# A decoder layer with 32 experts: tokens gathered for four experts at once, pairs combined by two-pass float32r products, and one branch moved

## The chip, the core and the metric

The kernel runs on one core of a Trainium2 chip. The metric is the time of one execution in microseconds (us); lower is better. TensorE (PE) multiplies matrices out of on-chip memory into PSUM, VectorE (DVE) and ScalarE (ACT) work element by element, GpSimd (POOL) does a few fills, and SyncE (SP) issues the transfers, which 16 DMA engines carry out.

## What is computed

One layer for 256 tokens of 1024 channels in float32. A token mixer with three groups of heads comes first, then a layer norm. After it come a mixture of experts, a gated embedding path, and a second layer norm:

```python
x = LN(alpha*x + mixer(x))
x = LN(alpha*x + MoE(x) + sigmoid(x W_g + b_g) * (p W_p))

logits = h @ w_router + b_router
top_v, top_i = lax.top_k(logits, 4)          # 4 of 32 experts for each token
gates = softmax(top_v)
gu = hb @ w_gate_up[e] + b_gate_up[e]        # hb: the tokens of expert e; 1024 -> 2048
g, u = min(gu[:, ::2], 7), clip(gu[:, 1::2], -7, 7)
act = (u + 1) * (g * sigmoid(1.702 * g))
y_e = act @ w_down[e] + b_down[e]            # 1024 -> 1024, added to the token, times its gate
```

Every expert's weights are read: 8 MB of w_gate_up and 4 MB of w_down each, 384 MB of the 431 MB that the kernel reads.

## The kernel before, in words

**The stream of weights.** SBUF has a ring of 22 slots of 1 MB (8 KB in each of 128 partitions, line 150). `want` queues units in the order of their use, `pump` gives a unit a slot as soon as one is free and issues its transfer from SP, and `done` frees a slot and pumps on. SP carries the transfers out in program order, so one that waits for a slot holds all that follow. An expert is 12 units: 8 of w_gate_up (`load_flat`, L245) and 4 of w_down (`load_rows2`, L224, for the last expert L231 and L239). Four slots are taken out of the ring for good (`room`, line 289: "act", "swi", "out", "acc"), and two more during experts 9 to 12, so that some 18 slots carry the stream.

**The mixer** (lines 264 to 940) fills the first 145 us. Its projections split float32 matrices exactly into two float32r parts (`split`, L406 and L407) and multiply the parts (L417 to L420, 256 columns a product; L788 to L790, 512 columns). The products of float32 operands elsewhere show as two records each. Its last part writes the normed stream `xn` (L861), finds each token's place among its expert's (`posm`, L918) and the gates `G` (`gates`, L924).

**The experts** (line 1271 on): one iteration e does up(e) and down(e - 1). Each expert has 64 slots for tokens. In an iteration, in the order of the code:

- the branch for more than 64 tokens at expert e (`over_up`, L1275), skipped by all experts but one;
- `expert_up(e)`: 32 float32 products of 512 columns (64 records, L1039), two blocks of columns side by side on the array; each row block of w_gate_up is released after use;
- the branch for the tokens past 64 of expert e - 1 (`over_down`, L1288), skipped likewise;
- at an even e `gather_gates` (L1003 to L1008): one-hots times gates, two transposes on TensorE, a copy; the result `CT` has the gates of two experts by slot and token;
- `expert_down(e - 1)` (32 records, L1066) into `y`, which holds a pair of experts in its two halves of partitions;
- `expert_act(e)`: copies out of PSUM (L1047, L1048), eight transposes (L1054) and the activation (`swiglu`, L1014 to L1020);
- at an even e `combine`: y of the finished pair times `CT`, four float32 products of 512 columns (8 records, L1028), each added to `yacc` by DVE (L1029);
- after it `gather` for the next pair: one-hots of posm (`Pm`, L986) multiplied with xn, 16 float32 products of 128 columns (32 records, L994), scaled out of PSUM in eight pieces by ACT and DVE (L966, L968) into `xe`, of which there are two buffers;
- in iterations 9 to 12 a quarter of the embedding path (`ple`, L1214 to L1226), which starts with 16 transposes of xn (L977);
- in iteration 4 `general()` (L1153): a branch for any counts, with loops inside. It is taken only above 96 tokens at an expert, and all engines skip it here.

The code's order is not quite the order of issue: within bounds each engine's list is ordered ahead of the run by readiness. After the last expert, its down runs by blocks of columns (`last_down`, L1336, and `last_combine`, L1345), and the second layer norm and the output follow.

Of the kernel before, what the change touches and what calls it, by code (L numbers as in the profile page):

```python
# [21 lines left out]
P = 128  # L22
# [19 lines left out]
GENERAL_AT = 4  # L42
NRUN = NE

# the table of shape constants: columns
# [11 lines left out]
# the packed small parameters: columns  # L57
# [49 lines left out]
def lay_out(inp):  # L107
    """The inputs as the launch takes them: small ones packed by partition, some transposed."""
# [18 lines left out]
    # ff = block * 256 + part * 128 + lane; column of w_gate_up = 2 * ff + (gate|up)  # L127
# [11 lines left out]
def kernel(ctx, tc, x, xT_in, pT_in, w_in, w_out, diff_lambda, params, bgu_in, w_gate_up,  # L139
# [9 lines left out]
    # ---- slots of 8 KB per partition: the stream of weights, and the mixer's larger intermediates  # L149
# [13 lines left out]
    def want(key, fn):  # L163
        pending.append((key, fn))

    def aside(fn):
        """fn() goes out in its place in the stream and takes no slot."""
        pending.append((None, fn))

    def pump():  # L170
        while pending and (free or pending[0][0] is None):
            key, fn = pending.pop(0)
            if key is None:
                fn()
                continue
            t, s = slot_tile()
            where[key] = s
            loaded[key] = fn(t)
# [28 lines left out]
    # ---- what the stream loads  # L207
# [56 lines left out]
    # ------------------------------------------------------------------ mixer  # L264
# [4 lines left out]
    def load_first_cols(u):  # L269
        """The first unit comes with xT, a quarter of each at a time."""  # L270
# [17 lines left out]
    # room that the experts need from then on, in places where the stream can spare it  # L288
    room = {3: "act", 5: "swi", 8: "out", 10: "acc"}
    n_want = RING  # L290
    for e in range(NRUN + 1):
# [20 lines left out]
        for key, fn in units:  # L312
            n_want -= 1
            if -n_want in room:
                key_ = room[-n_want]
                want(key_, lambda u: u)
# [60 lines left out]
    def keep_warm(n, warm, n_cols=512):  # L377
        """Products that nothing reads, so that the clock of the tensor engine stays up while it waits."""
# [21 lines left out]
    def split(half):  # L400
        """wh + wl = half of a unit exactly, each part with no more bits than a float32r has."""
# [46 lines left out]
    # output gates of groups A and C  # L448
# [12 lines left out]
    # ---- group A's gate of low rank: its 16 features in four parts, each the sum over a quarter of the channels  # L461
# [8 lines left out]
    # ---- group B's Toeplitz bias  # L470
# [12 lines left out]
    # ---- group A: gates, decays and scores of the gated linear attention  # L483
# [66 lines left out]
    # ---- group B: -lambda, scores and softmax  # L550
# [13 lines left out]
    def mixed(key, old, units):  # L564
        """Room for the high and low parts of two units of the mixed stream."""
# [21 lines left out]
    def diff_start(h, qz, kz):  # L587
        """A head's scores: each of its two maps has one half of the partitions."""
# [10 lines left out]
    def diff_softmax(h, t):  # L599
        """Both maps' weights of a tile of queries, and their difference."""  # L600
# [18 lines left out]
    def diff_turn(h, t):  # L619
        """The weights with keys along the partitions."""  # L620
# [7 lines left out]
    # ---- group C: retention scores  # L628
# [19 lines left out]
    def head_norm(o, po, blk, gcol):  # L648
        """o = po normed over a head's channels (po and o are channel by token)"""
# [31 lines left out]
    # ---- the rest of the projections, each group's work among those of the next  # L681
# [27 lines left out]
    # the router with the gain and bias of the layer norm: gain * w, and bias @ w + b  # L709
# [8 lines left out]
    # in each partition: -(the sum of an expert's weights), and its constant  # L718
# [54 lines left out]
    # expert e in each quarter of the partitions  # L773
# [3 lines left out]
    # ---- output projection, residual, first layer norm  # L777
# [24 lines left out]
    # xn is the normed stream without its gain and bias; x1T has both  # L802
    xn = cp.tile([P, NT, D], F32, name="xn")
# [3 lines left out]
    # the logits and four values above them all; the largest four, and four of those values  # L807
# [3 lines left out]
    nc.gpsimd.memset(lg[:, :, NE:], BIG)  # L811

# [458 lines left out]
    for e in range(NRUN + 1):  # L1271
# [10 lines left out]
        if e < 2:  # L1282
            bind(e)
# [103 lines left out]
```

## Time and profile before

| | |
|---|---|
| median of 3 runs (lowest to highest) | 1154.04 us (1151.01 to 1156.36) |
| span of the profiled execution, first to last instruction | 1148.8 us |
| TensorE, products | busy 1088.3 us, 95% |
| VectorE / ScalarE / GpSimd | 375.3 / 182.1 / 7.5 us (33% / 16% / 1%) |
| read from memory | 430.81 MB, 376 GB/s over the span |
| TensorE clock granted, mean | 0.981 |

The profile describes one execution, and this one's own time is its span; the median of the runs lies 5.2 us above the span, which holds what the runs have around it and their scatter. Busy time says how long an engine was in an instruction, not that it did its best. In a list of instructions over time, a line has the start, the length, the engine, the line of the kernel, the operation, output and input, the shape, a count, and in brackets how long the engine idled before and what ended that. An idle engine costs time only where its work is on the path to the end.

### The profile page before, as it was taken

What the parts mean: (1) busy time and instruction counts of PE and PEld (TensorE: products, weight loads), DVE (VectorE), ACT (ScalarE), POOL (GpSimd) and SP (SyncE); (2) the same over time, 40 slices, a digit from 0 to 9 for tenths busy, and PEclk for the clock granted to TensorE, in tenths of its full rate; (3) what the DMA queues carried; (4) which work ended last, traced back from release to release, by engine and by line L of the source; (5) the groups of instructions that cost most, each with busy time, mean ns of one, the idle gap of its engine ahead of it and who ended that gap; (6) DMA issues with size and microseconds to landing.
All of it is one profiled execution on the core that took longest, in us unless ns stands there. A gap on an engine that the chain in (4) does not pass through costs nothing. (4 is left out here: it accounts for less than half of the span.)

```text
span 1148.8 us, 14055 instructions
## 1 busy us (share of the span) xinstructions
PE 1088.3 (95%) x5566; PEld 548.7 (48%) x5566; DVE 375.3 (33%) x797; ACT 182.1 (16%) x372; POOL 7.5 (1%) x19
## 2 busy tenths in 40 slices
PE   9999999999699998999999999999998899999996
PEld 7888845434234344544534343434342433434334
DVE  4976632323023322411313132223232313222225
ACT  5457511101001111100101010101010100111001
POOL 1000000000000000000000000000000000000000
PEclk9999999999899999999999999999999898999999
DMA  9957888999799999999899999999999999999991
GB/s 319 361 220 265 336 344 338 405 402 416 302 416 417 416 407 407 398 360 388 331 416 416 415 415 417 415 416 416 416 415 417 416 417 417 393 417 416 415 347 38
DMA packets 100301, 433.64 MB, mean 377 GB/s; under 512 B 6957, under 2 KB 33325, under 8 KB 67409
## 3 DMA queue, kind: packets, MB, share of 16 engines
q1 hardware_dynamic: 100002, 431.36, 94.4%
q8 instruction: 90, 1.47, 0.5%
q0 software_dynamic: 176, 0.53, 0.1%
q14 instruction: 33, 0.27, 0.1%
HBM read 430.81 MB, written 1.06 MB: 376 GB/s over the span
## 5 line engine op out<-in xcount | busy, mean ns | idle before, releaser
L1039 PE MATMUL pgu<-u,xe 128*64 128x512 f32 x1024 | 242.1, 602 | 16.6 <-PEq L1288 9.9
L1039 PE MATMUL pgu<-u,u 128*64 128x512 f32 x1024 | 243.4, 604 | 5.8 <-PEq L1288 1.1
L1066 PE MATMUL py<-u,u 128*64 128x512 f32 x992 | 235.4, 602 | 5.7 <-DMA u<-in_w_down_dram 4.8
L1039 PEld LDWEIGHTS pgu<-u,xe 128*64 128x64 f32 x1024 | 85.5, 138 | 161.6 <-issue 149.7
L1039 PEld LDWEIGHTS pgu<-u,u 128*64 128x64 f32 x1024 | 89.7, 139 | 149.2 <-issue 139.0
L1048 DVE COPY u<-pgu 128x512 f32<-128x512 f32 x32 | 22.1, 692 | 392.9 <-PE pgu L1039 392.9
L1066 PEld LDWEIGHTS py<-u,u 128*64 128x64 f32 x992 | 80.6, 138 | 139.2 <-issue 121.7
L1014 DVE TENSOR_TENSOR u<-ptg,bgu 128x512 f32<-128x512 f32 x32 | 22.1, 692 | 219.8 <-PE ptg L1054 219.6
L1047 ACT COPY u<-pgu 128x512 f32<-128x512 f32 x32 | 18.8, 586 | 457.6 <-PE pgu L1039 457.6
L994 PEld LDWEIGHTS pgx<-Pm,xn 128*128 128x128 f32 x512 | 59.8, 192 | 8.3 <-issue 4.8
L994 PE MATMUL pgx<-Pm,xn 128*128 128x128 f32 x512 | 60.5, 275 | 1.0 <-PEq L1275 0.7
L1028 PE MATMUL pcb<-u,CT 128*128 128x512 f32 x120 | 57.5, 602 | 3.3 <-DVE u L1072 3.1
L1071 ACT COPY u<-py 64x512 f32<-64x512 f32 x31 | 17.9, 579 | 238.5 <-PE py L1066 238.5
L407 DVE TENSOR_TENSOR u<-u,u 128x1024 fp32r<-128x1024 f32 x32 | 39.1, 1223 | 17.1 <-ACT u L406 17.1
L1029 DVE TENSOR_TENSOR u<-u,pcb 128x512 f32<-128x512 f32 x64 | 43.5, 680 | 1.5 <-PE pcb L1028 1.5
L406 ACT CAST u<-u 128x1024 fp32r<-128x1024 f32 x32 | 33.5, 1048 | 29.9 <-PE pzt L418 9.6
L1028 PEld LDWEIGHTS pcb<-u,CT 128*128 128x128 f32 x120 | 20.6, 191 | 28.5 <-issue 14.1
L417 PE MATMUL pzt<-u,u 128*128 128x256 f32 x128 | 32.9, 291 | 0.0
L418 PE MATMUL pzt<-u,u 128*128 128x256 f32 x128 | 32.3, 287 | 0.0
L1214 PE MATMUL pleg<-u,u 128*128 128x256 f32 x128 | 29.8, 382 | 0.9 <-ACT u L1217 0.6
L1016 ACT ACTIVATE u<-u 128x512 f32<-128x512 f32 x32 | 20.2, 630 | 65.9 <-DVE u L1015 65.9
L1054 PEld LDWEIGHTS ptg<-ci,u 128*128 128x128 f32 x128 | 17.9, 207 | 26.3 <-issue 24.3
(277 smaller groups left out, 884.8 us busy)
## 6 DMA issues: line engine op xcount, KB each, us to landing
u<-in_w_gate_up_dram SPq DMA_DIRECT2D x256, 1024.0 KB, 16.7
u<-in_w_down_dram SPq DMA_DIRECT2D x127, 1024.0 KB, 17.6
u<-in_w_in_dram SPq DMA_DIRECT2D x11, 1024.0 KB, 12.9
u<-in_w_out_dram SPq DMA_DIRECT2D x4, 1024.0 KB, 11.0
u<-in_w_ple_gate_dram SPq DMA_DIRECT2D x4, 1024.0 KB, 17.8
u<-in_xT_dram SPq DMA_DIRECT2D x4, 256.0 KB, 4.1
u<-in_w_in_dram SPq DMA_DIRECT2D x4, 256.0 KB, 4.3
u<-in_w_in_dram SPq DMA_DIRECT2D x2, 512.0 KB, 7.2
```

The costliest lines, as they stand in the source:

```text
L406: nc.scalar.copy(wh, half)
L407: nc.vector.tensor_tensor(wl, half, wh.bitcast(F32), op=ALU.subtract)
L417: nc.tensor.matmul(pz[:, j, :], wh[:, k, :], xh[:, k, :], start=k == 0, stop=False)
L418: nc.tensor.matmul(pz[:, j, :], wh[:, k, :], xl[:, k, :], start=False, stop=False)
L994: nc.tensor.matmul(pg[:, j, :], xn[:, t, k * P:(k + 1) * P], Pm[:, t].rearrange("p e s -> p (e s)"), start=t == 0, stop=t == NT - 1)
L1014: nc.vector.tensor_tensor(g, pg, bg, op=ALU.add)
L1028: nc.tensor.matmul(pcb, CTp[:, t * P:(t + 1) * P], y[:, sl], start=True, stop=True)
L1029: nc.vector.tensor_tensor(yacc[:, t, sl], yacc[:, t, sl], pcb, op=ALU.add)
L1039: nc.tensor.matmul(pgu[b][hf * 64:(hf + 1) * 64, :], xe[:, k, c0:c0 + NSLOT], w[:, b * 1024 + hf * 512:b * 1024 + (hf + 1) * 512], start=k ...
L1048: nc.vector.tensor_copy(gs[:, 1, :], pgu[1])
L1066: nc.tensor.matmul(py[nb * 64:(nb + 1) * 64, :], act[:, j * 4 + blk, :], w[:, f % 2, nb * 512:(nb + 1) * 512], start=f == 0, stop=f == 7)
L1214: nc.tensor.matmul(pg[:, j, :], w[:, k, sl], x1T[:, k, :], start=k == 0, stop=k == NK - 1)
```

## The change

- `gather` works for groups: experts 0 and 1 as before, then four experts at a time (2 to 5, 6 to 9, ..., 26 to 29), and last 30 and 31. The one-hots are float32r; the normed stream is split once into `xnh` and `xnl` (float32r), and both are multiplied with the one-hots (256 columns a product). `xe` is one buffer for four experts. The gather of the next group stands after up(e) of a group's last expert.
- `gather_gates` stands ahead of expert_up(e) at an even e. It gives a one-hot `PT` (float32r) and a column `gate` in place of `CT`; the last pair keeps `CT`.
- `combine` of a pair becomes `weigh` (y times gate, split into `yh` and `yl`) in iteration e, and `combine_pair` (two float32r products for each of the four blocks) in iteration e + 1, after its up and gather. The combine in the branch and the last one stay.
- The transposes of `affine_transposed` become products of xnh and xnl with a float32r identity: 32 in place of 16.
- `xn` is `xs` normed in place; the slot of `xs` is freed after the split in iteration 0. `y` moves to the slot "swi", yh and yl take "out". The descriptor scratch of GpSimd's transfers shrinks from the default to 1024 bytes of a partition.
- `general()` goes from the end of iteration 4 to iteration 19, between the branch of expert 18 and down(18).

```diff
-GENERAL_AT = 4
+GENERAL_AT = 19
...
+    xnh = cp.tile([P, NT, D], F32R, name="xnh")
+    xnl = cp.tile([P, NT, D], F32R, name="xnl")
+    identr = cp.tile([P, P], F32R, name="identr")
+    nc.scalar.copy(identr, ident)
...
-            nc.scalar.activation(xn[:, t, sl], xs[:, t, sl], AF.Identity, scale=mv[:, 1:2], bias=nmr)
+            nc.scalar.activation(xs[:, t, sl], xs[:, t, sl], AF.Identity, scale=mv[:, 1:2], bias=nmr)
...
-                    nc.tensor.transpose(pt[:, k * P:(k + 1) * P], xn[:, t, (4 * q + k) * P:(4 * q + k + 1) * P], ident)
+                    ch = slice((4 * q + k) * P, (4 * q + k + 1) * P)
+                    for n, v in enumerate((xnh, xnl)):
+                        nc.tensor.matmul(pt[:, k * P:(k + 1) * P], v[:, t, ch], identr, start=n == 0, stop=n == 1)
...
+    def onehots(g):
+        n = size_of(g)
+        Pm = ep.tile([P, NT, n, NSLOT], F32R, name="Pm", tag="Pm", bufs=1)
+        sh = [P, NT, n, NSLOT]
...
+    def gather(g, Pm):
+        n = size_of(g) * NSLOT
+        w = 4 if g == 0 else 2
+        for q in range(NK // w):
+            pg = ps_s("pgx").rearrange("p (k s) -> p k s", k=w)
+            for j in range(w):
+                ch = slice((w * q + j) * P, (w * q + j + 1) * P)
+                for t in range(NT):
+                    hot = Pm[:, t].rearrange("p e s -> p (e s)")
+                    if g == 0:
+                        nc.tensor.matmul(pg[:, j, :n], xn[:, t, ch], hot.bitcast(F32), start=t == 0, stop=t == NT - 1)
+                        continue
+                    for i, v in enumerate((xnh, xnl)):
+                        nc.tensor.matmul(pg[:, j, :n], v[:, t, ch], hot, start=t + i == 0, stop=t + i == NT)
+            for j in range(w):
+                affine_evac(xe[:, w * q + j, :n], pg[:, j, :n], w * q + j, j % 2)
+
+    def split_stream():
+        for t in range(NT):
+            nc.scalar.copy(xnh[:, t], xn[:, t])
+            nc.vector.tensor_tensor(xnl[:, t], xn[:, t], xnh[:, t].bitcast(F32), op=ALU.subtract)
+        done("xs")
...
-        nc.vector.tensor_copy(CT, pct[:, :S])
-        return CT
+        if 2 * g + 2 == NRUN:
+            CT = ep.tile([P, S], F32, name="CT")
+            nc.vector.tensor_copy(CT, pct[:, :S])
+            return CT
+        PT = ep.tile([P, S], F32R, name="PT", tag="PT", bufs=2)
+        gate = ep.tile([P, 1], F32, name="gate", tag="gate", bufs=2)
+        nc.vector.tensor_scalar(PT, pct[:, :S], 0.0, None, op0=ALU.is_gt)
+        nc.vector.tensor_reduce(gate, pct[:, :S], axis=AX.X, op=ALU.add)
+        return PT, gate
...
+    def weigh(gate, y):
+        yh, yl = rm["yh"], rm["yl"]
+        for nb in range(2):
+            sl = slice(nb * 512, (nb + 1) * 512)
+            nc.scalar.activation(yh[:, sl], y[:, sl], AF.Copy, scale=gate)
+            nc.vector.scalar_tensor_tensor(yl[:, sl], y[:, sl], gate, yh[:, sl].bitcast(F32),
+                                           op0=ALU.mult, op1=ALU.subtract)
+        return yh, yl
+
+    def combine_pair(PT, ys):
+        yacc = rm["yacc"]
+        for t in range(NT):
+            for nb in range(2):
+                sl = slice(nb * 512, (nb + 1) * 512)
+                pcb = ps_s("pcb")
+                for i, v in enumerate(ys):
+                    nc.tensor.matmul(pcb, PT[:, t * P:(t + 1) * P], v[:, sl], start=i == 0, stop=i == 1)
+                nc.vector.tensor_tensor(yacc[:, t, sl], yacc[:, t, sl], pcb, op=ALU.add)
...
-            gs_of[e] = expert_up(e, st[e // 2][0])
+            if e % 2 == 0:
+                gates_of[e // 2] = gather_gates(e // 2, hot)
+            gs_of[e] = expert_up(e)
+        if e == 0:
+            split_stream()
+        if e + 1 < NRUN and group(e + 1) != group(e):
+            hot = onehots(group(e + 1))
+            gather(group(e + 1), hot)
         if e < 2:
             bind(e)
+        if weighed:
+            combine_pair(*weighed)
+            weighed = None
         if e == BIAS_AT:
             output_bias()
...
-        if e < NRUN and e % 2 == 0:
-            st[e // 2] = st[e // 2][0], gather_gates(e // 2, st[e // 2][1])
+        if e == GENERAL_AT:
+            general()
...
         if e >= 1 and f % 2 == 1:
-            combine(st.pop(f // 2)[1], y)
-        if (e == 1 or e % 2 == 0 and e > 0) and e + 2 < NRUN:
-            st[e // 2 + 1] = gather(e // 2 + 1)
+            PT, gate = gates_of.pop(f // 2)
+            weighed = PT, weigh(gate, y)
...
-        if e == GENERAL_AT:
-            general()
...
-    nc = bacc.Bacc("TRN2", target_bir_lowering=False, num_devices=1)
+    nc = bacc.Bacc("TRN2", target_bir_lowering=False, num_devices=1, dynamic_dma_scratch_size=1024)
```

## Rows read from the trace of the kernel before

**Rows 1.** The page's first part: busy time and share of TensorE's products and the others.

```profile
PE 1088.3 (95%) x5566; PEld 548.7 (48%) x5566; DVE 375.3 (33%) x797; ACT 182.1 (16%) x372; POOL 7.5 (1%) x19
```

**Rows 2.** Stretches: length, busy time of the engines, granted clock, DMA share, GB/s.

```profile
150.00:200.00 50.00, 48.27 (x235) 24.18 (x237) 12.89 (x28) 5.36 (x11) 1.81 (x1) 1.00 0.88 331
200.00:280.00 80.00, 77.12 (x346) 32.53 (x342) 20.32 (x37) 6.58 (x12) 0.00 (x0) 0.98 1.01 406
280.00:320.00 40.00, 29.86 (x140) 13.33 (x140) 8.52 (x19) 3.61 (x7) 0.00 (x0) 0.87 0.82 335
320.00:480.00 160.00, 154.58 (x729) 73.00 (x729) 48.78 (x96) 19.35 (x40) 0.00 (x0) 1.00 1.02 412
480.00:580.00 100.00, 93.41 (x420) 48.15 (x420) 21.42 (x39) 8.20 (x16) 0.00 (x0) 0.97 0.92 364
...
820.00:900.00 80.00, 71.42 (x315) 26.84 (x314) 18.04 (x35) 6.58 (x12) 0.00 (x0) 1.00 1.02 416
...
980.00:1000.00 20.00, 19.59 (x102) 10.30 (x99) 8.61 (x17) 3.04 (x6) 0.00 (x0) 1.00 0.96 384
1000.00:1100.00 100.00, 98.43 (x432) 40.33 (x429) 23.51 (x44) 11.35 (x20) 0.00 (x0) 0.98 1.02 416
1100.00:1120.00 20.00, 19.70 (x82) 7.50 (x82) 5.55 (x10) 0.59 (x1) 0.00 (x0) 1.00 0.96 320
```

**Rows 3.** TensorE in order of time, over one pair of experts (up 18 to up 20).

```profile
700.35 15.11 PE L1039 MATMUL pgu<-u,u 128*64 128x512 f32 x64
...
723.84 1.02 PE L1028 MATMUL pcb<-u,CT 128*128 128x512 f32 x2
725.12 2.81 PE L1028 MATMUL pcb<-u,CT 128*128 128x512 f32 x6 [0.26 <-DVE u L1072]
727.77 3.73 PE L994 MATMUL pgx<-Pm,xn 128*128 128x128 f32 x32
731.65 14.68 PE L1039 MATMUL pgu<-u,u 128*64 128x512 f32 x63
...
754.93 7.52 PE L1039 MATMUL pgu<-u,xe 128*64 128x512 f32 x34
```

**Rows 4.** The end: SP's last loads, and TensorE's next to last block of columns.

```profile
1109.38 5.68 SPq L239 DMA_DIRECT2D u<-in_w_down_dram  x2
...
1133.97 1.15 PE L1336 MATMUL pyl<-u,u 128*64 128x64 f32 x32
```

**Rows 5.** The mixer's float32r products in order of time: 256 columns, then 512.

```profile
20.43 0.28 PE L418 MATMUL pzt<-u,u 128*128 128x256 f32 x1
...
20.55 0.28 PE L417 MATMUL pzt<-u,u 128*128 128x256 f32 x1
...
121.04 0.39 PE L788 MATMUL pw<-u,u 128*128 128x512 f32 x1
...
121.27 0.39 PE L789 MATMUL pw<-u,u 128*128 128x512 f32 x1
```

**Rows 6.** TensorE, the first 12 of the embedding path's 16 transposes of xn.

```profile
429.72 1.85 PE L977 MATMUL ptx<-ci,xn 128*128 128x128 f32 x12
```

**Rows 7.** The mixer's splits by line: count, busy us, mean ns, idle before.

```profile
L407 DVE TENSOR_TENSOR u<-u,u 128x1024 fp32r<-128x1024 f32 x32 | 39.1, 1223 | 17.1 <-ACT u L406 17.1
L406 ACT CAST u<-u 128x1024 fp32r<-128x1024 f32 x32 | 33.5, 1048 | 29.9 <-PE pzt L418 9.6 <-DMA u<-in_w_in_dram 7.4 <-PE pw L789 6.1
```

**Rows 8.** TensorE after general() was skipped: up(5).

```profile
296.77 15.76 PE L1039 MATMUL pgu<-u,xe 128*64 128x512 f32 x64 [9.88 <-PEq L1288]
```

**Rows 9.** Experts 5 and 6: the last transposes, the activation's last step, the gates.

```profile
319.91 0.64 PE L1054 MATMUL ptu<-ci,u 128*128 128x128 f32 x4
...
324.24 0.69 DVE L1020 TENSOR_TENSOR u<-u,u 128x512 f32<-128x512 f32 x1
...
336.46 0.41 DVE L1008 COPY CT<-pct 128x256 f32<-128x256 f32 x1
...
336.79 0.42 DVE L1003 TENSOR_TENSOR Cm<-Pm,G 128x256 f32<-128x256 f32 x1
```

More of the change, by code (lines that the diff above doesn't have):

```diff
@@ L175, in pump @@
                 continue
-            t, s = slot_tile()
+            t, s = slot_tile(dtype)
             where[key] = s
@@ L315 @@
                 key_ = room[-n_want]
-                want(key_, lambda u: u)
+                want(key_, lambda u: u, F32R if key_ == 'out' else F32)
             want(key, fn)
@@ L910 @@
     done("m1")
-    done("xs")
+    xn = xs
     nc.tensor.matmul(ppos[:, 0:NE], tri, mb[:, 0, :], start=True, stop=True)
@@ L945 @@
     placed = [None]
-    xe0 = ep.tile([P, NK, 2 * NSLOT], F32, name="xe0")
+    xe = ep.tile([P, NK, 4 * NSLOT], F32, name="xe")
     def bind(e):
         if e == 1:
-            rm["y"], rm["yo"] = carve(loaded["out"], (D,), (D,))
+            rm["yh"], rm["yl"] = carve(loaded["out"], (D,), (D,))
             rm["yacc"] = loaded["acc"].rearrange("p (t d) -> p t d", t=NT)
@@ L980, in affine_transposed, with group @@
         return x1T
-    def gather(g):
-        Pm = ep.tile([P, NT, 2, NSLOT], F32, name="Pm", tag="Pm", bufs=1)
-        sh = [P, NT, 2, NSLOT]
-        placed[0] = nc.vector.tensor_tensor(Pm, iota[:, None, None, :NSLOT].to_broadcast(sh),
-                                            posm[:, :, 2 * g:2 * g + 2, None].to_broadcast(sh), op=ALU.is_equal)
-        xe = rm["xe1"] if g % 2 else xe0
-        for q in range(2):
-            pg = ps_s("pgx").rearrange("p (k s) -> p k s", k=4)
-            for j in range(4):
-                k = 4 * q + j
-                for t in range(NT):
-                    nc.tensor.matmul(pg[:, j, :], xn[:, t, k * P:(k + 1) * P],
-                                     Pm[:, t].rearrange("p e s -> p (e s)"), start=t == 0, stop=t == NT - 1)
-            for j in range(4):
-                affine_evac(xe[:, 4 * q + j, :], pg[:, j, :], 4 * q + j, j % 2)
-        return xe, Pm
+    def group(e):
+        return 0 if e < 2 else 1 + (e - 2) // 4
@@ L1080, in over_gather @@
             for t in range(NT):
-                nc.tensor.matmul(px[:, k, :NOVER], xn[:, t, k * P:(k + 1) * P], Po[:, t, :],
-                                 start=t == 0, stop=t == NT - 1)
+                for i, v in enumerate((xnh, xnl)):
+                    nc.tensor.matmul(px[:, k, :NOVER], v[:, t, k * P:(k + 1) * P], Po[:, t, :],
+                                     start=t + i == 0, stop=t + i == NT)
         xo = ep.tile([P, NK, NOVER], F32, name="xo", tag="xo")
@@ L1253, in broadcast_ln2 @@
             nc.scalar.copy(u[:, sl], pl)
-    st = {}
     y = None
-    st[0] = gather(0)
-    n_of = {}
+    hot = onehots(0)
+    gather(0, hot)
+    n_of, gates_of = {}, {}
     gs_of, act_of, ov_of = {}, {}, {}
+    weighed = None
     def count(e):
```

33 lines of the change are left out of this document (21 added, 12 removed).

## The prediction

> **What bounds the kernel now.** The first part of the page shows TensorE busy for 95% of the span and no other engine above 33% [rows 1]. That alone doesn't say that TensorE sets the time, so the second view is the table of stretches [rows 2], read from its last column: the reader is to see that the loads run at 416 GB/s wherever nothing holds them (820 to 900 us, 1000 to 1100) and never faster in a long stretch, and that the granted clock is 1.00 while TensorE waits for them (820 to 900). At 416 GB/s an expert's 12.58 MB take 30.25 us and a pair's 60.5 us. The third view is TensorE over one pair [rows 3]: from up(18) at 700.35 to up(20) at 754.93 us it works back to back, 54.6 us. So in the steady part TensorE is the quicker of the two, and the loads ought to set the pace.
>
> They don't from the start. At 150 us the ring is full, because the mixer used the loads more slowly than they came; a load then starts only when TensorE frees a slot, and each pause of TensorE is one of the stream. I count what the stream lost against 416 GB/s: 150 to 200 us (1 - 331/416) x 50 = 10.2 us; 200 to 280 1.9; 280 to 320 7.8; 320 to 480 1.5; 480 to 580 (the embedding path) 12.5; 980 to 1000 1.5 [rows 2]. Together 35.4 us, of which 25.2 after 200 us. In 1100 to 1120 us 6.4 MB were left, 15.4 us, so the stream ends near 1115.4; SP's last loads are issued at 1109.38 and landing fits [rows 4]. From there the kernel takes 33 us to its end at 1148.8, because TensorE has fallen behind again. The bound is thus mixed: the stream, its holes, which TensorE makes, and a tail on TensorE.
>
> **Gather, part by part.** One gather of a pair takes TensorE 3.88 us, from 727.77 to 731.65 [rows 3]. After gather(0), which stays, there are 15: 58.2 us. Afterwards there are 8, each of 32 products of 256 columns in float32r; the mixer's products of that shape follow each other by 0.12 us [rows 5], so 3.8 us each. The last one has 128 columns a product, which no row shows for float32r; the float32 gather's 32 records of 128 columns in 3.73 us bound it above at twice that, if each product costs two records, 7.5 us, and half of 0.12 us a product below, 1.9 us; I take 3.8. Sum 30.4, saved 27.8 us.
>
> **Combine.** It holds TensorE from 723.84 to 727.77, 3.93 us, a wait for y's copy included [rows 3]. 15 of them move to the new form: 59.0 us. Afterwards each has eight products of 512 columns at 0.23 us [rows 5]: 1.8 us, 27 in all, saved 32.0 us. It comes an iteration later, so the wait goes too. The Trainium skill (TensorE: Matmul & The Clock Gate, Back-to-back issue gap) gives about 131 ns for 512 columns in a sustained stream; a combine of 1.0 us is the estimate by that page. The row shows 0.23 us, and it decides.
>
> **Beside other work.** `weigh` adds two copies on ACT and two subtractions on DVE for each pair, about 0.7 us each (the 512-column step on DVE took 0.69) [rows 9], and has the 15 us of the next up to hide in [rows 3]; DVE is 33% busy [rows 1]. If that cover went, the combine would wait up to 2.8 us. The one-hot and the sum in place of one copy of 0.41 us add the like of one more such pass on DVE, with a whole up before they are needed. Eight pieces out of PSUM serve four experts instead of two, so ACT and DVE gain there. The split of the stream, two copies of 1.05 and two subtractions of 1.22 us [rows 7], runs on two engines beside up(0), a stretch like the 15 us of up(18) [rows 3]; without that cover it would hold gather(1) by up to 4.5 us. The slot of xs comes free later: at worst one load, 2.5 us of the stream, nothing at best, since the stream stands waiting there anyway (331 GB/s) [rows 2]; I take nothing. The transposes for the embedding path took 12 in 1.85 us, so 2.5 for 16 [rows 6]; 32 products cost between 1.9 and 7.5 us by the bounds above, and I take 0.12 each as for the 256 columns, since each needs a weight load of the same size: +1.3 us. The smaller scratch touches two small transfers in the mixer; I take nothing, and bound it by 2 us either way.
>
> **The branch.** Skipping general() leaves TensorE idle for 9.88 us [rows 8], at the end of iteration 4, when the ring is full: the stream loses 7.8 us there [rows 2]. At expert 19 the pause comes again. I take its TensorE time as the same 9.9 us, but let it cost the stream nothing, because TensorE then keeps up with the stream: the ring's 18 slots are 45 us of loads, and the pause fills a quarter of them. SP skips the branch too, with loads already issued in flight; a stream that stood as long as at expert 4 would cost 7.8 us, the upper end.
>
> **The sum.** TensorE gets 27.8 + 32.0 - 1.3 = 58.5 us less to do, 4 us a pair: 50.5 against the stream's 60.5. Up to up(5) alone it is ahead for good by the branch, 9.9, by one gather, 3.9, and by what one combine saves, 2.1: 15.9 us, so the hole at 280 to 320 us goes. Then it gains 10 us a pair on the stream until it waits for loads, and the embedding path, whose hole was 12.5 us in all, finds free slots. Of the 25.2 us I keep 3.0 (320 to 480 and 980 to 1000 us, the second after the branch of the one overfull expert). The stream ends at 1115.4 - 22.2 = 1093.2 us. TensorE, with 58.5 us less, is through up(31) by then, waiting for loads, and what is left after the last load is the next to last block and all behind it: 1148.8 - 1133.97 = 14.8 us [rows 4]. Span 1093.2 + 14.8 = 1108 us. The median of the runs shown is 5.2 us above the profiled span (1154.04 against 1148.8), so **1113 us**.
>
> **Rivals.**
> (A) This forecast, 1100 to 1122: at 1100 all 35.4 us of holes vanish (1115.4 - 35.4 + 14.8 + 5.2); at 1122 the branch costs the stream its 7.8 us and the unknown terms another one.
> (B) The stream doesn't end sooner. Where it ran at 416 GB/s, freeing TensorE brings nothing, and if the holes have other causes (code loading, SP's own order, the embedding path's loads), they stay: only the tail shrinks, 1115.4 + 14.8 + 5.2 = **1135 us**. For it: the stream is full in most stretches [rows 2]. Against it: the holes lie where TensorE paused or had extra work. The Trainium skill (Perfetto Trace Analysis, Identifying the Most-Contended Engine) says that busy time of matmuls is a bad measure, that the loads are judged by their rate, and that the most contended resource is the one to work on; by that rule this change turns the wrong screw, which is this case. The trace agrees in the steady part and not before 320 us.
> (C) A float32r product costs half of a float32 one, as one of its two records does: eight products of 0.43 us are 3.4 us a combine, 32 of 0.24 are 7.5 us for a gather of four. TensorE saves only half a microsecond a pair, and the time stays within 0.5%, near **1150**. Against it stand the mixer's 0.12 and 0.23 us [rows 5].
> (D) Slower: `gather_gates` now stands ahead of up(e), and on DVE its first step, one-hots times gates (`Cm`), stands behind the activation of the expert before. If it is issued there, TensorE idles from the end of the transposes (319.91 + 0.64) to the end of the activation (324.24 + 0.69) and 0.42 for the step: 4.8 us [rows 9], at 15 pairs 72 us, with everything in up(e) queued behind. A pause also lowers the clock: 0.87 over the stretch around the branch [rows 2], where up(5) took 15.76 against 15.11 us [rows 8, 3]; 15 times 0.65 is 9.8. 1148.8 + 72 - 58.5 + 9.8, less the 8.6 us that TensorE waited for loads in 820 to 900 [rows 2], is 1163.5 and with 5.2 **1169 us**. It decides from 3.9 us a pair on (58.5 over 15). Against it: `Cm` of the pair to come was issued 0.33 us after the copy of the pair before [rows 9], two iterations ahead of its place in the code, since its inputs are there; the same can happen now.
>
> **How the numbers follow.** A 0.64, B 0.20, C 0.07, D 0.09. Likeliest is A, 1113 us. The range runs from 1099 to 1140 and holds A and B with a few microseconds for their unknown terms; it leaves out 0.16. A change within 0.5%, 5.8 us, can't be told from none. Faster is A and B, 0.84; same is C, 0.07; slower is D, 0.09.
>
> **What would show it.** Right: a combine of 1.8 us and a gather of 3.8 us for four experts on TensorE; 400 GB/s or more in every stretch from 200 us to the last load; many short waits of TensorE for loads after expert 8; the last load near 1093 us and 15 us after it; a pause of some 10 us in iteration 19 without a dip of the rate. B shows as the same dips with TensorE waiting; C in the steps of the products; D as 5 us of idle before each even up, ended by DVE. The prediction is wrong if the span is over 1135, or if TensorE still works back to back past expert 20.

## The result, and the profile after

The kernel after takes **1135.61 us** (median of 4 runs, 1132.45 to 1138.67), the kernel before beside it 1155.2 us; the ratio is 0.984, 95% interval 0.982 to 0.986. Forecast was 1113 us, with a range of 1099 to 1140. So the sign and the range hold, and some 20 of the forecast 41 us are there. The profiled execution has a span of 1132.3 us against 1148.8: 16.5 us less, where 41 were worked out.

First the page's busy times, the answer to [rows 1]. TensorE has 49.7 us less to do, DVE and ACT a little more:

```profile
PE 1038.6 (92%) x5358; PEld 515.0 (45%) x5358; DVE 396.5 (35%) x809; ACT 194.1 (17%) x377; POOL 7.5 (1%) x19
```

Then the stretches of [rows 2], each a separate part of the span, with the same columns (length; busy time of PE, PEld, DVE, ACT, POOL; granted clock; DMA share; GB/s):

```profile
150.00:200.00 50.00, 44.32 (x211) 18.37 (x212) 12.76 (x23) 7.29 (x12) 1.80 (x1) 0.97 0.77 297
200.00:280.00 80.00, 76.22 (x334) 30.05 (x335) 24.45 (x46) 7.35 (x12) 0.00 (x0) 0.98 1.02 416
280.00:320.00 40.00, 37.37 (x188) 17.05 (x190) 16.48 (x31) 5.38 (x10) 0.00 (x0) 1.00 1.02 416
320.00:480.00 160.00, 147.97 (x692) 71.25 (x690) 45.61 (x83) 20.35 (x37) 0.00 (x0) 0.98 1.02 411
480.00:580.00 100.00, 91.42 (x430) 45.99 (x428) 28.72 (x50) 10.76 (x19) 0.00 (x0) 0.98 1.02 414
...
820.00:900.00 80.00, 63.30 (x280) 25.21 (x280) 20.68 (x38) 9.32 (x20) 0.00 (x0) 0.94 1.02 417
900.00:980.00 80.00, 75.48 (x408) 29.42 (x402) 23.98 (x50) 8.58 (x16) 0.00 (x0) 0.93 0.98 399
...
1000.00:1100.00 100.00, 95.77 (x446) 39.99 (x444) 29.37 (x54) 14.01 (x24) 0.00 (x0) 1.00 1.02 410
1100.00:1120.00 20.00, 18.58 (x192) 12.15 (x194) 9.37 (x20) 3.47 (x7) 0.00 (x0) 1.00 0.29 86
```

From 200 us on the stream is as forecast: the holes of 335 and 364 GB/s are gone. Two things are not. Between 150 and 200 us the rate is lower than before (297 against 331 GB/s: 14.3 us lost against 10.2). And at the end 86 GB/s in the last full stretch are 1.7 MB, so the stream ends at about 1104 us, while the kernel ends 28 us later. TensorE's idle time by line says where it waits now:

```profile
L1127 PE MATMUL py<-u,u 128*64 128x512 f32 x992 | 234.9, 605 | 27.8 <-DVEq L1361 18.0 <-DMA u<-in_w_down_dram 4.2 <-ACT u L1108 3.0
L1041 PE MATMUL pct<-ci,Cm 128*128 128x128 f32 x32 | 7.0, 300 | 13.8 <-DVE u L1133 10.3 <-PEq L1338 3.2
```

The 18.0 us are new (13 waits): a pair's combine now stands right ahead of the branch of `over_down`, L1361. DVE adds four blocks of 0.68 us to `yacc` and passes the branch after them, and `down` waits until it has. In the kernel before the combine was followed by the gather, whose 3.7 us of products covered the adds. The 10.3 us (10 waits of 1.03) stand ahead of an even expert's up, where the gates' transposes wait for DVE's copy of y.

Last, TensorE in order of time around the overfull expert 25, with the clock in five short stretches:

```profile
891.10 0.40 PE L1143 MATMUL pox<-Pr,xnh 128*128 128x32 f32 x1 [5.42 <-DVE Pr L965]
...
898.58 9.69 PE L1166 MATMUL pgo<-u,xo 128*32 128x512 f32 x64 [0.47 <-ACT xo L972]
908.98 0.74 PE L1174 MATMUL pto<-ci,gso 128*128 128x128 f32 x4 [0.72 <-ACT gso L1169]
909.65 2.79 PE L1100 MATMUL pgu<-u,xe 128*64 128x512 f32 x12
```

```profile
886.00:891.00 5.00, 0.00 (x0) 0.00 (x0) 4.83 (x10) 1.24 (x2) 0.00 (x0) 0.92 1.01 419
891.00:896.00 5.00, 4.90 (x23) 4.90 (x24) 0.19 (x2) 0.00 (x0) 0.00 (x0) 0.50 1.02 414
896.00:901.00 5.00, 4.53 (x22) 2.59 (x26) 0.00 (x0) 2.26 (x8) 0.00 (x0) 0.50 1.01 411
901.00:906.00 5.00, 5.00 (x40) 1.30 (x36) 0.00 (x0) 0.00 (x0) 0.00 (x0) 0.71 1.02 402
906.00:911.00 5.00, 4.28 (x36) 1.47 (x30) 1.21 (x5) 0.84 (x2) 0.00 (x0) 1.00 1.04 424
```

TensorE ends the transposes of expert 24 at 885.67 us, then waits 5.42 us for the one-hot of the overflow tokens, which DVE reaches only after the activation and the new weighing. After the pause the granted clock is 0.50, 1.2 GHz, and the products of `pox` take 7.0 us (4.40 in the kernel before). The Trainium skill (TensorE: Matmul & The Clock Gate, What's actually happening) says that the throttled state is the default and that activity releases it; these rows agree, with 0.50 at the end of the pause and 1.00 again in the last stretch. up(25) starts at **909.65** us, 24.0 us after the transposes.

This start splits the span, and what follows hangs on that split. Before: 924.33 us, and 224.5 us from there to the end. After: 909.65 and 222.6. So **14.7 of the 16.5 us came ahead of up(25), and 1.8 behind it**.

### The profile page after: what moved, and what is told of

It reads as the page before. It is cut to its first block, busy times and chain, and to the rows that moved or that the text cites. A ratio compares the mean times of both kernels' runs of the same rounds, so it can differ in the third digit from the quotient of the medians.

```text
span 1132.3 us, 13655 instructions
## 1 busy us (share of the span) xinstructions
PE 1038.6 (92%) x5358; PEld 515.0 (45%) x5358; DVE 396.5 (35%) x809; ACT 194.1 (17%) x377; POOL 7.5 (1%) x19
## 5 line engine op out<-in xcount | busy, mean ns | idle before, releaser
L1100 PE MATMUL pgu<-u,xe 128*64 128x512 f32 x2048 | 475.5, 604 | 15.4 <-DMA u<-in_w_gate_up_dram 8.9
L1100 PEld LDWEIGHTS pgu<-u,xe 128*64 128x64 f32 x2048 | 161.1, 139 | 307.1 <-issue 271.4
L1132 ACT COPY u<-py 64x512 f32<-64x512 f32 x31 | 17.9, 578 | 277.7 <-PE py L1127 277.7
L1090 DVE TENSOR_TENSOR u<-u,pcb 128x512 f32<-128x512 f32 x60 | 37.7, 682 | 13.9 <-PE pcb L1089 13.8
L1089 PE MATMUL pcb<-u,PT 128*128 128x512 f32 x120 | 32.0, 408 | 0.0
L1022 PE MATMUL pgx<-Pm,xnh 128*128 128x256 f32 (+1 forms) x128 | 30.9, 284 | 0.0
L1022 PE MATMUL pgx<-Pm,xnl 128*128 128x256 f32 (+1 forms) x128 | 30.0, 278 | 0.0
L1276 PEld LDWEIGHTS pleg<-u,u 128*128 128x128 f32 x128 | 24.9, 199 | 6.3 <-ACT u L972 2.2
L1022 PEld LDWEIGHTS pgx<-Pm,xnh 128*128 128x128 f32 x128 | 24.1, 188 | 6.5 <-issue 4.1
L1089 PEld LDWEIGHTS pcb<-u,PT 128*128 128x128 f32 x120 | 21.0, 188 | 11.7 <-ACT u L1108 4.9
```

Of the source, the lines that this page charges most:

```text
L1022: nc.tensor.matmul(pg[:, j, :n], v[:, t, ch], hot, start=t + i == 0, stop=t + i == NT)
L1089: nc.tensor.matmul(pcb, PT[:, t * P:(t + 1) * P], v[:, sl], start=i == 0, stop=i == 1)
L1090: nc.vector.tensor_tensor(yacc[:, t, sl], yacc[:, t, sl], pcb, op=ALU.add)
L1100: nc.tensor.matmul(pgu[b][hf * 64:(hf + 1) * 64, :], xe[:, k, c0:c0 + NSLOT], w[:, b * 1024 + hf * 512:b * 1024 + (hf + 1) * 512], start=k ...
L1276: nc.tensor.matmul(pg[:, j, :], w[:, k, sl], x1T[:, k, :], start=k == 0, stop=k == NK - 1)
```

## The experiments

All runs were timed beside the kernel before. Two of the theories that the expectations name fell on the way; they are numbered as they came. Theory 1: the gain is lost in TensorE's new waits. Theory 2: the stream sets the end. Theory 3: the moved branch costs it. Theory 4, formed after e8: the span is the start of up(25) plus what TensorE has left from there, and a change is worth what it does to one of the two.

| run | median, us | ratio (95%) | up(25) starts | from there to the end |
|---|---|---|---|---|
| before | 1152 to 1155 | 1 | 924.3 | 224.5 |
| after | 1135.6 | 0.984 (0.982 to 0.986) | 909.7 | 222.6 |
| e1 combine last | 1144.1 | 0.993 (0.990 to 0.995) | 910.0 | 230.9 |
| e2 e1, gates behind up | 1133.4 | 0.983 (0.982 to 0.985) | 902.7 | 231.1 |
| e3 no overfull branch | 1125.1 | 0.977 (0.975 to 0.980) | | |
| e4 no general() | 1135.7 | 0.984 (0.982 to 0.987) | 910.7 | 224.7 |
| e5 early one-hot | 1135.0 | 0.983 (0.980 to 0.985) | 909.0 | 227.6 |
| e6 both in mid up | 1138.8 | 0.987 (0.985 to 0.989) | 910.9 | 226.3 |
| e7 e5 and e6 | 1135.1 | 0.986 (0.982 to 0.989) | 908.4 | 222.3 |
| e8 float32 combine | 1138.7 | 0.988 (0.986 to 0.989) | 907.6 | 226.7 |
| e9 before, branch at 19 | 1151.4 | 0.998 (0.996 to 1.000) | 925.4 | 224.8 |
| e10 first gates behind up(0) | 1130.0 | 0.981 (0.979 to 0.983) | 904.6 | 224.4 |
| e11 e10, LN2 sooner | 1125.6 | 0.978 (0.976 to 0.980) | 903.3 | 218.9 |
| **e12 e5, e6, e11** | **1120.7** | **0.973 (0.971 to 0.975)** | 899.7 | 219.0 |
| e13 after, branch at 4 | 1136.3 | 0.987 (0.983 to 0.990) | 911.6 | 221.2 |
| e14 gather twice | 1151.7 | 0.998 (0.996 to 1.000) | 922.6 | 230.8 |
| e15 e14 and e8 | 1158.5 | 1.004 (1.002 to 1.006) | 921.1 | 233.9 |

The last two columns are of the profiled executions (start of the first product of up(25); span less that). One execution lies up to 3.6 us off the median of its kernel, e5's and e14's profiled ones some 3.5 us above it, so differences of 2 to 3 us in these columns can be scatter.

**e1 and e2: the order.** The combine goes from ahead of the branch to the end of the iteration; in e2 the gates go behind up as well.

```diff
-        if weighed:
-            combine_pair(*weighed)
-            weighed = None
...
             act_of[e] = expert_act(e, gs_of.pop(e))
+        if weighed:
+            combine_pair(*weighed)
+            weighed = None
```

> The pair's combine is moved from ahead of the branch of the expert before (and of its down) to the end of the iteration, behind the activation. Theory 1 (the order): TensorE's 13 waits for DVE's branch (18.0 us in all) go, since DVE's adds no longer stand between TensorE and the branch; the part of them behind the overfull expert's branch, some 4 combines with 1.4 us and what they delay, comes off the end: 1126 to 1131 us. The adds then stand behind the activation and ahead of Cm, so the waits ahead of the even experts' up may grow from 1.0 us. Theory 2 (the stream): what is lost is the stream's (its early holes, the xs slot), TensorE's waits only fill time: 1134 to 1137 us. Theory 3 (the branch for any counts at expert 19): no change either, 1134 to 1137 us.

> Combine to the end of the iteration as in the run before this, and the gates' transposes (Cm, pct) moved from ahead of an even expert's up to behind it. Theory 1: both waits go (18.0 us ahead of down, 10.3 us ahead of up over the kernel; of these some 5.6 and 3.1 us behind the overfull expert's branch): 1122 to 1128 us. Theories 2 and 3: 1134 to 1137 us.

e1 is 8 us slower than the kernel after, which no theory wanted. The gates, ahead of up, now stand behind the adds, and in e2, where they don't, their own work stands ahead of the branch. One line of each kernel's groups:

```profile
L1041 PE MATMUL pct<-ci,Cm 128*128 128x128 f32 x32 | 7.2, 310 | 19.6 <-DVE u L1090 17.9 <-PEq L1338 0.9 <-DVE u L1059 0.6
```

```profile
L1127 PE MATMUL py<-u,u 128*64 128x512 f32 x992 | 233.4, 608 | 36.3 <-DVEq L1358 27.2 <-DMA u<-in_w_down_dram 7.6 <-DVE u L1109 0.8
```

The wait doesn't go away, it moves: 17.9 us ahead of the gates in e1, 27.2 us at the branch in e2 (20 waits). Whatever gives DVE work shortly ahead of a point where TensorE needs DVE is waited for here. This shows why nothing is won, but not where e1's 8 us come from: they lie behind up(25) (230.9 us against 222.6), and TensorE's waits there are 9.6 us against 10.2. Its products there are busy for 209.9 us in place of 201.8. The granted clock is 0.50 for some 14 us of that stretch against 7, worth about 3.4 us by estimate; the rest stays open. e2 shows something else, used below: its up(25) starts 7 us sooner.

**e3 and e4: leaving out a branch.** In e3 the overfull expert's condition is never true; in e4 `general()` is gone.

```diff
-            with tc.If(n_of[e] > NSLOT):
+            with tc.If(n_of[e] > S - 1):
```

> The branch's condition is never true, so the tokens past the 64th of the overfull expert 25 are left out (its up, down and combine of the overflow); all else stands. Theory 1 (TensorE can't catch up behind that branch): 24 us before up(25) and some 9 us behind it leave TensorE, which then waits for loads to the end; the stream ends at 1098 to 1101 us and the tail is the 15 us that it was in the old kernel: 1115 to 1120 us. Theory 2 (the tail hangs on the stream, not on TensorE): the tail stays 28 us, 1130 to 1136 us.

> The branch for any counts, not taken with these inputs, is left out (counts above 96 are then not served). Theory 1: its 8 to 10 us of TensorE at expert 19 are given back by waits for loads between 820 and 885 us: 1134 to 1137 us. Theory 3: the 8 to 10 us are lost for good: 1125 to 1128 us.

e4 settles theory 3: the moved branch costs nothing. The pause is there in the kernel after (at expert 19: 3.04, 2.16 and 2.67 us of idle time; in e4 1.23 and 1.03 are left), but the stream stays at 416 GB/s from 580 to 820 us, and TensorE has waits for loads from which it pays. e3 gains 10.5 us, less than the 16 to 21 of theory 1. There the bound by loads does come back: behind 885 us TensorE waits 26 times for loads of gate_up, where the kernel after has no such wait behind up(25), and the tail is short. First these waits (us in all, number, longest), then TensorE at the end:

```profile
PE pgu L1100 <- DMA u<-in_w_gate_up_dram: 15.0, 26, 1.3
```

```profile
1102.96 1.97 PE L1406 MATMUL pyl<-u,u 128*64 128x128 f32 x32 [0.30 <-DMA u<-in_w_down_dram]
...
1108.90 1.15 PE L1406 MATMUL pyl<-u,u 128*64 128x64 f32 x32
```

From the last line to the end are 14.9 us, the 14.8 of [rows 4]. So the 28 us behind the last load of the kernel after are there because TensorE is late from the overfull expert on.

**e5 to e8: taking the waits away, and giving the products back.** e5 makes the one-hot for every expert ahead of the activation. e6 has the combine (odd experts) or the gates (even) in the middle of up. e7 has both. e8 has float32 combines of four passes.

```diff
+            po_ = over_pos(e + 1)
+            nxt = po_, over_hot(po_)
             act_of[e] = expert_act(e, gs_of.pop(e))
```

```diff
             w = loaded["gu", e, k]
+            if k == 4:
+                midway()
```

> The one-hot of the overflow slots (Pr) is made for every expert ahead of the activation of the expert before, outside the branch, so pox no longer waits behind the activation and the weighing. Theory 1 (now: what counts is TensorE's work from the overfull expert's branch on): the wait of 5.42 us goes, and if it is this pause that drops the granted clock to 0.50 for some 14 us after it, pox (32 in 6.8 us, 4.4 us in the old kernel) and part of pgo get shorter too; 7 to 10 us in all, 1125 to 1129 us. Theory 2 (the stream sets the end): 1134 to 1137 us.

> The pair's combine stands in the middle of an odd expert's up (ahead of its channel block 4 of 8) in place of behind it, the gates' transposes in the middle of an even expert's up in place of ahead of it: DVE's adds and gates then run beside the second half of up. Theory 1: the waits for DVE's branch (13 times, 18.0 us) and for the copy of y ahead of the gates (10.3 us) go; only those behind expert 25's branch count, 4 with 1.4 us and 3 with 1.0 us: 1125 to 1130 us. Theory 2: 1134 to 1137 us.

> Both edits. Theory 1: the two gains add, 14 to 18 us, until the stream (it ends at about 1104 us in the kernel after) and 15 us behind it set the end: 1116 to 1122 us. Theory 2: 1134 to 1137 us.

> The kernel after, with the pair's combine by float32 products as before (8 become 4 of four passes, no weighing, the gates' transpose kept in float32), in the same place. TensorE gets 15 times 3.9 less 2.1 us, 27 us in all. Theory 1: only the four behind expert 25's branch, with 1.8 us each, count, 7 us, less about 1.5 us as weighing no longer stands ahead of pox: 1139 to 1144 us. If every combine counted: 1160 us and more. Theory 2: 1134 to 1137 us.

Theory 1 falls here: three kernels with fewer waits gain nothing. The table shows why for e5 and e7: up(25) starts at 909.0 and 908.4 us although `pox` starts up to 2.6 us sooner and takes 4.82 and 3.72 us in place of 7.0. `pgo`, which needs all eight blocks of up(25)'s weights, then waits for loads (3.29 us in e5, 4.28 in e7). The stream was just behind the wait that was taken away. It was also 2 to 3 us later than in the kernel after: between 150 and 200 us it ran at 270 GB/s in e5 and 279 in e7, in place of 297. Kernels whose edits stand far behind that stretch have 273 and 276 there (e13, e4), so this much is scatter between the kernels, and e5 and e7 show only a part of the missing gain to be the loads'. The fall of the clock doesn't hang on the pause, as the expectation of e5 supposed it might: without the pause the granted clock is 0.50 from 892 to 898 us in e5, from the middle of `pox` on, and from 894 to 897 in e7.

What is behind up(25) didn't shrink either: e5 and e6 have 5.0 and 3.6 us more there than the kernel after, though their waits there are 9.8 and 3.7 us against 10.2. The products are busy for 206.8 and 211.0 us in place of 201.8. The granted clock is 0.50 for some 17 us of that stretch in both, against 7, worth about 5 us by estimate; the rest of e6's stays open. e8 gives 27 us of products back and costs 3.0 us by the medians, at the edge of what the two intervals can tell apart: by the profiled executions the price is 4.1 us behind up(25) and nothing ahead of it, a little under what theory 1 had, and theory 4 keeps this.

**e9 to e12: testing theory 4.** The kernel after stalls for 3.70 us in front of up(1); two products of up(1) have been put between the transposes of expert 0 there. In the run with the gates moved (e2) this was gone. So e10 moves only the first pair's gates behind up(0). Here is TensorE at that place, first in the kernel after, then in e10:

```profile
165.22 1.04 PE L1100 MATMUL pgu<-u,xe 128*64 128x512 f32 x2 [0.29 <-DMA u<-in_w_gate_up_dram]
166.19 0.62 PE L1115 MATMUL ptg<-ci,u 128*128 128x128 f32 x3
166.65 0.28 PE L1115 MATMUL ptu<-ci,u 128*128 128x128 f32 x1
170.63 0.59 PE L1115 MATMUL ptu<-ci,u 128*128 128x128 f32 x2 [3.70 <-issue]
```

```profile
166.52 0.52 PE L1115 MATMUL ptu<-ci,u 128*128 128x128 f32 x3
167.53 4.94 PE L1100 MATMUL pgu<-u,xe 128*64 128x512 f32 x22 [0.49 <-DMA u<-in_w_gate_up_dram]
```

```diff
-            if e % 2 == 0:
+            if e % 2 == 0 and e:
                 gates_of[e // 2] = gather_gates(e // 2, hot)
             gs_of[e] = expert_up(e)
+            if e == 0:
+                gates_of[0] = gather_gates(0, hot)
```

e11 also has `LN2_AT = 20`, and e12 adds e5 and e6. e9 is the kernel before with `GENERAL_AT = 19`.

> The kernel before with the branch for any counts moved from the fourth expert's iteration to the twentieth's, nothing else. Theory 4 (the time is the start of up(25), which the stream's holes before 870 us set, plus what TensorE has left from there): the hole of 280 to 320 us (335 GB/s in place of 416, 7.8 us) goes, up(25) starts 5 to 8 us sooner, the rest stays 224 us: 1146 to 1150 us. Theory 1 (what counts is TensorE's own time, and the branch's 10 us stand now at expert 19): no change, 1152 to 1156 us.

> The kernel after with the first pair's gates alone moved from ahead of up(0) to behind it, as in the run with both moves, where TensorE's stall of 3.70 us in front of up(1) was gone, the stream's hole between 150 and 200 us was 8.3 us in place of 14.4, and up(25) started at 902.66 in place of 909.65 us. Theory 4: up(25) starts 5 to 7 us sooner, the rest stays 222 to 226 us: 1127 to 1131 us. Theory 1 (only TensorE's waits behind expert 25 count): 1134 to 1137 us.

> The same, and the second layer norm's broadcast (8 products, 3.7 us) eight experts... that is seven iterations sooner, at expert 21's iteration in place of 28's, where TensorE waits for loads. Theory 4: those 3.7 us leave the part behind up(25): 1123 to 1128 us, unless the slot that its load keeps from then on costs the stream something. Theory 1 as well as theory 4 want this gain, a bound by the stream to the end wants none: 1127 to 1131 us.

> Combine and gates in the middle of up, the early one-hot, the first pair's gates behind up(0), the broadcast sooner. Theory 4: the start of up(25) at 901 to 904 us, as gate_up(25) can't land sooner; the rest 222 us less 3.7: 1120 to 1126 us. Theory 1 (each wait taken away counts): 1112 to 1118 us.

e10, e11 and e12 come out as theory 4 has them, 1130.0, 1125.6 and 1120.7 us (e11 was wanted by theory 1 as well, and e12's up(25) starts 1.3 us ahead of its range). In e10 the rate from 150 to 200 us is 338 GB/s in place of 297, which is 4.9 us of stream; up(25) starts 5.1 us sooner:

```profile
150.00:200.00 50.00, 47.54 (x240) 22.80 (x238) 17.48 (x34) 8.42 (x14) 1.80 (x1) 1.00 0.88 338
```

Among the runs that leave what lies just ahead of up(25) as it is, up(25) roughly follows the rate of this stretch: 902.7 us at 348 GB/s (e2), 904.6 at 338 (e10), 909.7 at 297 (the kernel after), 911.6 at 273 (e13). So a pause of TensorE at 167 us is paid at 910 us, since nothing between gives the stream anything back. In e11 the 3.7 us of the broadcast leave the part behind up(25), which shrinks by 5.5 us (224.4 to 218.9). In e12, e5's and e6's edits, worth nothing by themselves, are worth 5 us; that it is because the stream now comes sooner is argued, not tried. And `pgo` again ends on loads:

```profile
884.73 6.56 PE L1173 MATMUL pgo<-u,xo 128*32 128x512 f32 x40 [0.47 <-ACT xo L972]
892.07 1.06 PE L1173 MATMUL pgo<-u,xo 128*32 128x512 f32 x8 [0.78 <-DMA u<-in_w_gate_up_dram]
894.57 1.06 PE L1173 MATMUL pgo<-u,xo 128*32 128x512 f32 x8 [1.44 <-DMA u<-in_w_gate_up_dram]
897.07 1.06 PE L1173 MATMUL pgo<-u,xo 128*32 128x512 f32 x8 [1.43 <-DMA u<-in_w_gate_up_dram]
```

e12 is the fastest version here, 1.1% below the kernel after by the two ratios. e9 missed, and theory 1's "no change" was right about it. Its hole at 280 to 320 us is gone (416 GB/s), but the pause comes again ahead of up(20), with 3.90 us more behind its first product:

```profile
757.52 1.08 PE L1039 MATMUL pgu<-u,xe 128*64 128x512 f32 x1 [8.54 <-PEq L1288]
762.51 13.04 PE L1039 MATMUL pgu<-u,xe 128*64 128x512 f32 x52 [3.90 <-issue]
```

```profile
820.00:900.00 80.00, 78.73 (x360) 32.80 (x361) 22.38 (x44) 7.49 (x14) 0.00 (x0) 1.00 1.02 417
```

TensorE of the kernel before idles for 8.6 us between 820 and 900 us [rows 2], 7.1 of them in waits for loads; here 1.3 are left, none of them for loads. What the stream gained at 300 us, TensorE lost at 750, and up(25) starts where it did.

**e13 to e15: which part made the gain.** e13 has `GENERAL_AT = 4` in the kernel after. e14 does every product group of a gather twice, and e15 has the float32 combine as well.

```diff
-            for j in range(w):
+            for j in [j for j in range(w) for _ in range(2 if g else 1)]:
```

> The kernel after with the branch for any counts back at the fourth expert. Theory 4: the hole at 280 to 320 us is back (7 to 8 us), nothing gives it back since the kernel is bound by the stream from there to 885 us, up(25) starts 6 to 8 us later, the rest stays: 1140 to 1145 us. Rival (the place of the branch is worth nothing, as in the kernel before): 1134 to 1137 us.

> The kernel after with each gather of four (32 float32r products, 3.9 us) done twice, the second over the first, so that the gather costs TensorE about what the old ones did, 31 us more in all. Theory 4: ahead of expert 25 the 23 us hide, since TensorE waits for loads there; behind it the two gathers count, 7.7 us: 1141 to 1146 us. If every product counted: 1160 us and more. If none did (the stream sets all): 1134 to 1137 us.

> That and the combine by float32 products: TensorE has about as much to do as in the kernel before, with the branch at the twentieth expert and the new order. Theory 4: behind up(25) 7.7 and 4 us more than in the kernel after, and ahead of it TensorE, at some 58 us for a pair of experts where the stream takes 60.5 us, no longer gets back what its pauses at 150 to 200 us and at the branch cost, so that up(25) starts 3 to 10 us later: 1148 to 1156 us. If the cheaper products ahead of expert 25 are worth nothing: 1144 to 1148 us.

e13: the rival was right, the branch's place is worth nothing in this kernel either. The skip itself costs less in this run, where it stands ahead of `down` and not at the iteration's end: 0.56 and 2.57 us of TensorE, where up(5) waited 9.88 [rows 8], and the stream runs on. The place within the iteration alone doesn't make it cheap: at expert 19, in the same place, it is 7.04 us in one piece in e14. Here is e13:

```profile
278.48 7.23 PE L1127 MATMUL py<-u,u 128*64 128x512 f32 x32 [0.56 <-PEq L1215]
...
289.43 3.61 PE L1100 MATMUL pgu<-u,xe 128*64 128x512 f32 x9 [2.57 <-PEq L1338]
```

```profile
280.00:320.00 40.00, 35.87 (x173) 17.71 (x171) 10.87 (x19) 5.67 (x10) 0.00 (x0) 0.96 1.02 416
```

e14 costs 16 us by the medians, more than theory 4 wanted, and the split of its profiled execution, which is 21 us longer than the kernel after's, says where it was wrong: behind up(25) it is 8.2 us, as expected (two gathers, 7.7), but up(25) also starts 13 us later. The products of the gather ahead of it don't all hide; the stream has holes again where TensorE has most to do, at the start and in the embedding path:

```profile
150.00:200.00 50.00, 44.15 (x218) 20.04 (x220) 12.08 (x22) 6.72 (x11) 1.80 (x1) 0.93 0.70 259
...
480.00:580.00 100.00, 93.44 (x429) 48.63 (x428) 24.56 (x43) 8.80 (x16) 0.00 (x0) 0.97 0.99 388
```

e15 costs 6.8 us more than e14 by the medians, and is 2.5 us above what theory 4 wanted. Its profiled execution is only 1.6 us longer than e14's, so the split doesn't show where the 6.8 us are. So of the some 19 us that the change gained, the cheaper gather is worth most: giving its time back costs 16 us, giving the combine's time back 3 to 7 (the 3 barely clear of scatter), moving the branch back nothing. With both given back the kernel is at 1158.5 us, 0.4% above the kernel before.

## Why the prediction was right and wrong

**The prices held.** A gather for four takes 3.87 us (923.54 to 927.41; 3.8 was forecast) and the last one, with 128 columns, 3.63, so the bound that counted half a product was the wrong end. A combine holds TensorE for 2.14 us against 1.8: 5 us over the kernel. By these rows TensorE is held some 53 us less, where 58.5 were forecast. The forecast set the Trainium skill's 131 ns for 512 columns (TensorE: Matmul & The Clock Gate, Back-to-back issue gap) against a row of 0.23 us; the row came near, for the eight products step by 0.25 us. The same section has N / 2.4 + 2.5 ns for a single product, an estimate of 216 ns here, which is the one that these rows come near.

**The stream from 200 to 900 us held.** By the stretches 2.4 us of the holes are left between 200 and 900 us. The rate is 411 to 417 GB/s in each, and TensorE waits for loads between 820 and 885 us as forecast. The reason given for it held. The prediction gave the branch 9.9 of the 15.9 us that close the hole at 280 to 320 us, and the branch's move closes it by itself in the kernel before (e9, 416 GB/s); in the kernel after it stays closed with the branch at expert 4 too, where the skip takes 3.1 us (e13). The hole of the embedding path, 480 to 580 us, is the gather's: 368 GB/s with the branch moved alone (e9), 414 in the kernel after, 388 with the gather done twice (e14) and 413 with the float32 combine (e8).

**The branch at expert 19** costs the stream nothing, as taken, and TensorE idles 7.9 us around it where 9.9 were forecast. That this made a gain against its old place was wrong (e9, e13).

**The xs slot and the start.** "I take nothing" for 0 to 200 us was wrong: 2.5 us more are lost up to 150 us (298 GB/s in place of 305) and 4.1 between 150 and 200, with the stall at up(1) that e10 removes. That part the prediction hadn't seen at all. The 2.5 us, though just the upper end that was set for xs, aren't shown to be its slot's: e9, which frees xs as the kernel before does, has 299 GB/s there. Behind 200 us it kept 3.0 us of holes; by the stretches it is 2.4, and 4.7 more behind 900 us (399 and 410 GB/s). Together 10.7 us, and the stream ends at 1104 and not at 1093.2 us.

**The step that failed** is: "TensorE, with 58.5 us less, is through up(31) by then, waiting for loads, and what is left after the last load is the next to last block". The average rate of a pair was used for a stretch that has its own limit. From the overfull expert on TensorE doesn't wait for loads: its branch can't end before all of up(25)'s weights are there (e7, e12), and up(25) begins only then, where other experts' up runs along with its loads. Behind it stand 222.6 us, of which all but some 11 are TensorE's products and waits. Here is all from the start of up(25) on, first before, then after:

```profile
924.30:1200.00 275.70, 210.53 (x1085) 90.59 (x1084) 67.59 (x137) 22.17 (x44) 0.00 (x0) 0.97 0.72 290
```

```profile
909.60:1200.00 290.40, 201.84 (x1094) 88.02 (x1092) 75.60 (x149) 26.58 (x50) 0.00 (x0) 0.97 0.69 276
```

The products are busy for 8.7 us less, and 8.1 us come back as waits (10.2 in place of 2.1). Of the 8.7 the change's own products give about 3.5 (four combines of 2.14 us in place of three of 4.0; two gathers in place of two about as long). Most of the rest is up of experts 25, 27, 29 and 31, 13.95 us each in place of 15.1; why was not tried. The forecast left 14.8 us behind the last load; it is 28. The prediction named two signs against itself. The span, 1132.3 us, isn't over 1135; but from up(25) on, past expert 20, TensorE works without a wait for loads.

So the span misses by 24 us (1132.3 against 1108): 11 by the stream's end and 13 by the tail. That e3, without the overfull expert's branch, has waits for loads again and a tail of 14.9 us shows the tail's part; which of TensorE's work in it could go is shown only for the broadcast (e11).

**Of the rivals,** B named the measured number, 1135, by another mechanism: the stream does end 11 us sooner, and the tail keeps 28 of its 33 us. C was wrong by the prices above. D's place was right and its price wrong: `Cm` is there in time, and the wait ahead of an even up is 1.03 us for the copy of y, not 4.8. The prediction had asked what is queued behind the gates, and not what DVE owes when it comes to the next branch; that wait, 18.0 us, wasn't on its list.

## What to carry to other kernels

Find the last point at which the limit changes hands, and value an edit by what it does on either side of it; a saving per iteration is not a saving of the span. Ahead of such a point a wait can be worth nothing because the stream is just behind it (e5, e7), and worth 5 us once the stream comes sooner (e12). Nor did the products behind it take the same time in every kernel: 201.8 to 211.0 us for the same work, in part by the granted clock, so that a wait taken away there didn't show in the span (e6). The Trainium skill (Perfetto Trace Analysis, Optimization Strategy) says that a kernel can have several regimes with different most contended engines; here the regime changes at an expert that the data choose.

Where work is moved, look at what stood behind it: the gather had covered the adds of the combine, and the order after the change put a branch there, at which TensorE waits for whatever DVE still has to do.

## What was not expected of the hardware

- The granted clock fell to 0.50 at the end of the 5.42 us pause, and 32 products of 32 columns took 7.0 us there against 3.72 in e7 without the pause. It fell without the pause as well, in the middle of these products (e5) or just behind them (e7).
- The cost of a skipped branch depends on where it stands: 9.88 us of TensorE at the end of iteration 4, 0.56 and 2.57 us in the middle of the same iteration (e13), 7.04 us in the middle of iteration 19 (e14). Why was not tried.
- Moving two small transposes (the gates of the first pair) took away a stall of 3.70 us that the profile lists as "issue", at another place. The order of issue shows two products of up(1) among the transposes there in the kernel after; that this causes the stall is argued from the order, and not tried by itself.
